# The first pairs of a squared-ReLU MLP: which sum's product comes first, where the low parts stand, and where the third pair's first product and its copy stand

## The chip, the core and the metric

The kernel runs on one core of a Trainium2 chip. The metric is the device time of one execution, in microseconds (us); lower is better. The core has a matrix engine (TensorE, PE in the profile), a vector engine (VectorE, DVE), a scalar engine (ScalarE, ACT), GpSimd (POOL) and SyncE (SP), which here only issues transfers. Each engine works through its own list of instructions; where one needs another's result it waits at that place in its list.

## What is computed

One layer of a diffusion trunk for 640 tokens (128 of a prompt, 512 latent) of width 1024: a token mixer with three head groups, then an MLP. The change lies in the MLP's first half:

```python
x = _layernorm(ALPHA * x + g1 * m, lp['ln1_g'], lp['ln1_b'])
hid = jnp.square(jax.nn.relu((x * (1.0 + sc2) + sh2) @ lp['w_ff1']))
x = _layernorm(ALPHA * x + g2 * (hid @ lp['w_ff2']), lp['ln2_g'], lp['ln2_b'])
```

`w_ff1` is 1024 x 4096 in float32. Rounding has to stay near that of float32, so every operand is split into a rounded high part and a low part (what is left), and a product of two operands is three matmuls: high by high, high by low, low by high.

## The kernel before

**The tiling.** The 4096 hidden columns are worked in 16 pairs (`u` = 0 to 15) of 256. A pair is a 2 x 2 product of blocks: the tokens in two halves of 320 (`HALF`), the 1024 inputs in two halves of 512, the hidden columns in two blocks of 128. Instead of eight block products the kernel forms seven, with sums of blocks on either side (Winograd's form): `m1` = a11 b11, `m2` = a12 b21, `m6` = s2 t2, `m5` = s1 t1, `m7` = s3 t3, `m4` = a22 t4, `m3` = s4 b22. The a's are the four quarters of the modulated, transposed input (`raws`, tiles q00 to q11); s1 to s4 are sums of quarters and are formed once, in the first pairs. The b's are quarters of a pair's weights and t1 to t4 their sums (`b_sums3` and `b_sum4`, lines 1315, 1316 and 1320), formed anew for each pair. A product is 12 matmuls (`prod`, line 1461): four blocks of 128 inputs, three terms each.

**The results.** Products add up in PSUM: m1, m6, m7, m4 of a pair in its bank x, m2 in bank y, m5 and m3 in bank z. Between them ScalarE copies bank x aside, since each of its partial sums is used (`keep(u, 1)` after m1, `keep(u, 2)` after m6, `keep(u, 3)` after m7; line 1467). The next product into x can't begin before that copy has read the bank. `c11`, `c22`, `c21`, `c12` add a bank and a copy (`out_sum`, line 1480, VectorE) and apply the squared ReLU (`relu2`, lines 1472 and 1473 on ScalarE, line 1475 on VectorE).

**Splitting.** ScalarE rounds the high part and VectorE subtracts it for the low one: `hi_(u, what, lo, hi)` (line 1343) and `lo_` (line 1347) for weights, where what = 1 is b11, 2 is b21 and b22 (in that order), 3 is t1, t3, t2, t4 (in that order; `lo` and `hi` pick some of them); `sum_hi` (line 1284) and `sum_lo` (line 1287) for the a's and s's. The program's names in the profile are those of buffers: pairs alternate between two sets, and wf12h and wf12l are the even and the odd pair's b's, wf3h and wf3l the high and low parts of the t's, wf_t the t's before the split, wf_r the loaded weights.

**The order.** From the second half of the output projection on, the order of TensorE, ScalarE, VectorE and SyncE is written out by hand: each of them executes its instructions in the order in which the program text issues them. The lines ahead of the loop `for u in range(2, NU)` are such a list for the pairs 0 and 1 and the beginning of pair 2: m1(0) and m2(0) while the last 128 tokens are still normalized and transposed (`normalize(4)`, `turn(4)`, `h2(4, ...)`, lines 1279 and 1281 for the scaling), then m1(1), m2(1), the sums s1 and s2 and their splits, m6(0), m5(0), m6(1), m5(1), then s3, m7(0), m7(1), and so on to m3(1). In the loop of pair u stand, in this order: `m1(u)`, `keep(u, 1)`, the t's of pair u+1 (`b_sums`), `hi_(u+1, 1)`, m4 and m3 of pair u-1, `lo_(u+1, 1)`, the other splits of pair u+1 with `hi_(u+1, 3)` last, `m2(u)`, `c11(u)`, `m6(u)`, `keep(u, 2)`, `lo_(u+1, 3)`, `m5(u)`, `m7(u)`, `keep(u, 3)`. For u = 2 there is no m4 and m3 of pair 1 (they stand in the list ahead).

**Loads.** `load(u)` reads a pair's weights by SyncE into one of two tiles, w0 and w1, once the tile's former reader is done; s1 (`s1r`) and s2 (`s2r`) lie in these two tiles at first, so load(2) waits for the last reader of `s1r` and load(3) for that of `s2r`. Finished blocks of hidden values are parked in DRAM by GpSimd (`store`).

Of the kernel before, what the change touches and what calls it, by code (L numbers as in the profile page):

```python
# [33 lines left out]
HALF = NTOK // 2  # L34
# [23 lines left out]
def f32(ap):  # L58
    return ap.bitcast(F32)
# [3 lines left out]
def hybrid_layer_kernel(ctx: ExitStack, tc: tile.TileContext, T):  # L63
    nc = tc.nc
    V, A, G, PE = nc.vector, nc.scalar, nc.gpsimd, nc.tensor
# [928 lines left out]
    gr, parts, tok, wks = {}, {}, {}, {}  # L994
# [203 lines left out]
    def parts(*names):  # L1198

        for n in names:  # L1200
            t = sps.tile([P, 2, 4, HALF], F32R, tag=n, name=n)
            sums[n] = [t[:, 0], t[:, 1]]
# [59 lines left out]
    def turn(t, bank="f", qs=(0, 1)):  # L1262

        for q in qs:
            pst[t, q] = fps[0].tile([P, 512], F32, tag=bank, name=f"psh{t}{q}")
            for k in range(4):
                kk = q * 4 + k
                PE.transpose(pst[t, q][:, k * P : (k + 1) * P], xn[:, t, kk * P : (kk + 1) * P], ident)

    def h2(t, q, *which):  # L1270

        v = 1 if t == 0 else 0
        spans = ((0, 64, 0, 256), (64, 64, 1, 0)) if t == 2 else ((0, P, t // 3, t * P - t // 3 * HALF),)
        for o, n, th, c0 in (spans[i] for i in which or range(len(spans))):
            for k in range(4):
                kk = q * 4 + k
                dst, src = raws[th, q][:, k, c0 : c0 + n], pst[t, q][:, k * P + o : k * P + o + n]
                if q and t:
                    V.tensor_scalar(dst, src, a2[:, kk, v : v + 1], b2[:, kk, v : v + 1], op0=ALU.mult, op1=ALU.add)
                else:  # L1280
                    A.activation(dst, src, AF.Identity, scale=a2[:, kk, v : v + 1], bias=b2[:, kk, v : v + 1])

    def sum_hi(n, src, lo=0, hi=HALF):
        A.copy(sums[n][0][:, :, lo:hi], src[:, :, lo:hi])

    def sum_lo(n, src, lo=0, hi=HALF):
        V.tensor_tensor(sums[n][1][:, :, lo:hi], src[:, :, lo:hi], f32(sums[n][0][:, :, lo:hi]), op=ALU.subtract)
# [18 lines left out]
    def b_sums(u, pool, tag):  # L1306

        b_sums3(u, pool, tag)
        b_sum4(u)

    def b_sums3(u, pool, tag):
        g = U[u]
        r = g.r
        g.t = t = pool.tile([P, 4, 4, P], F32, tag=tag, name=f"wf_t{u}")
        V.tensor_tensor(t[:, 0:2], r[:, :, :, 1, :], r[:, 0].rearrange("p k c n -> p c k n"), op=ALU.subtract)
        V.tensor_tensor(t[:, 2], r[:, 1, :, 1, :], t[:, 0], op=ALU.subtract)

    def b_sum4(u):
        g = U[u]
        V.tensor_tensor(g.t[:, 3], g.r[:, 1, :, 0, :], g.t[:, 2], op=ALU.subtract)  # L1320
# [20 lines left out]
    def hi_(*a):  # L1341
        h, l, src = part(*a)
        A.copy(h, src)  # L1343

    def lo_(*a):
        h, l, src = part(*a)
        V.tensor_tensor(l, src, f32(h), op=ALU.subtract)  # L1347
# [22 lines left out]
    for t in range(NT):  # L1370
        ps = wo_gemm(t, 0, wk)
# [18 lines left out]
    for t in range(NT):  # L1390
        ps = wo_gemm(t, 1, wk, "y" if t == 4 else "f")
# [59 lines left out]
    def banks(u):  # L1451
        U[u].ps = {b: fps[0].tile([P, 512], F32, tag=b, name=f"ps{b}{u}") for b in "xy"}

    def prod(u, b, sn, wn, start):

        ps = U[u].ps[b][:, 0:HALF]
        sh, sl = sums[sn]
        wh, wl = U[u].w[wn]
        for k in range(4):
            for i, (a_, b_) in enumerate(((wh, sh), (wh, sl), (wl, sh))):  # L1460
                PE.matmul(ps, a_[:, k, :], b_[:, k, :], start=start and k == 0 and i == 0, stop=k == 3 and i == 2,  # L1461
                          skip_group_check=True)

    def keep(u, i):

        t = kept[:, (3 * u + i - 1) % 6, :]
        A.copy(t, U[u].ps["x"][:, 0:HALF])  # L1467
        setattr(U[u], f"s{i}", t)
# [14 lines left out]
    def m1(u):  # L1483
        prod(u, "x", "a11", "b11", True)

    def m2(u):
        prod(u, "y", "a12", "b21", True)

    def m6(u):
        prod(u, "x", "s2", "t2", False)  # L1490

    def m5(u):
        U[u].ps["z"] = fps[0].tile([P, 512], F32, tag="z", name=f"psz{u}")
        prod(u, "z", "s1", "t1", True)

    def m7(u):
        prod(u, "x", "s3", "t3", False)
# [4 lines left out]
    def m3(u):  # L1502
        prod(u, "z", "s4", "b22", False)
# [4 lines left out]
    def c22(u):  # L1508
        out_sum(u, "z", U[u].s3, 1, 1, False)
# [6 lines left out]
    def c12(u):  # L1516
        out_sum(u, "z", U[u].s2, 1, 0, True)
        store(u, 1)
# [20 lines left out]

    s1r, s2r, s3r = (wop.tile([P, 4, HALF], F32, tag=f"w{i}", name=f"s{i + 1}r") for i in range(3))  # L1540

    def sums12(lo, hi):
        c = slice(lo, hi)
        V.tensor_tensor(s1r[:, :, c], raws[1, 0][:, :, c], raws[1, 1][:, :, c], op=ALU.add)
        V.tensor_tensor(s2r[:, :, c], s1r[:, :, c], raws[0, 0][:, :, c], op=ALU.subtract)

    banks(0)
    banks(1)
    m1(0)
    turn(3, qs=(1,))  # L1550
    m2(0)
    h2(2, 0, 1)
    turn(3, qs=(0,))
    lo_(1, 1)
# [1 line left out]
    lo_(1, 2, 0, 1)  # L1556
    normalize(4, mvs[4])
    turn(4, "z")
    h2(3, 0)
    h2(4, 0)  # L1560
    h2(4, 1)
    m1(1)
    m2(1)
    keep(0, 1)
    keep(1, 1)
    sums12(0, 192)
    parts("s2")
    sum_hi("s2", s2r, 0, 192)
    hi_(1, 3, 2, 3)
    sums12(192, HALF)  # L1570
    sum_lo("s2", s2r, 0, 192)
    sum_hi("s2", s2r, 192)
    sum_lo("s2", s2r, 192)
    parts("s1")
    sum_hi("s1", s1r)
    sum_lo("s1", s1r)
    load(2, wop, "w0")
    lo_(1, 3, 2, 3)
    hi_(1, 3, 0, 2)
    hi_(1, 3, 3, 4)  # L1580
    hi_(1, 2, 1, 2)
    m6(0)
    keep(0, 2)
    m5(0)
    V.tensor_tensor(s3r, raws[0, 0], raws[1, 0], op=ALU.subtract)
    sums["s3"] = [rawp.tile([P, 4, HALF], F32R, tag=f"q{i}0", name=f"s3{i}") for i in range(2)]
    sum_hi("s3", s3r)
    lo_(1, 3, 0, 2)
    lo_(1, 2, 1, 2)
    m6(1)  # L1590
    keep(1, 2)
    m5(1)
    sum_lo("s3", s3r)
    lo_(1, 3, 3, 4)
    m7(0)
    parts("a22")
    sum_hi("a22", raws[1, 1])
    sum_lo("a22", raws[1, 1])
    hi_(2, 1)
    hi_(2, 2, 0, 1)  # L1600
# [16 lines left out]
    c22(1)  # L1617
    lo_(2, 1)
    m3(1)
    b_sums3(2, wop, "w2")  # L1620
    hi_(2, 3, 2, 3)
    lo_(2, 3, 2, 3)
    lo_(2, 2, 0, 1)
    c12(0)
    hi_(2, 3, 0, 2)
    c11(1)
    store(1, 0)
    lo_(2, 3, 0, 2)
# [3 lines left out]
    lo_(2, 3, 3, 4)  # L1632
    hi_(2, 2, 1, 2)
    lo_(2, 2, 1, 2)

    def pair(w, gh, gl, raw, rows_):

# [12 lines left out]
    for u in range(2, NU):  # L1650
        more = u + 1 < NU
        gate = None
        banks(u)
        if u + 2 < NU:
            load(u + 2, wop, f"w{u % 2}")
        elif more:
            raw0 = wop.tile([P, 2, 512], F32, tag="w0", name="wg0_r")
            ff2_raw(raw0, NF - 4, 0)
        m1(u)
        keep(u, 1)  # L1660
        if u > 2:
            c22(u - 1)
        if more:
            b_sums(u + 1, wop, "w2")
            hi_(u + 1, 1)
        else:
            early = sps.tile([P, 1024 + 2 * NTOK], F32, tag="a11", name="early")
            raw1 = early[:, 0:1024].rearrange("p (k n) -> p k n", n=512)
            ff2_raw(raw1, 0, 0)
            for i in range(2):  # L1670
                nc.sync.dma_start(early[:, 1024 + i * NTOK : 1024 + (i + 1) * NTOK], parked[i])
        if u > 2:
            m4(u - 1)
            c21(u - 1)
            m3(u - 1)
        if more:
            lo_(u + 1, 1)
            hi_(u + 1, 2)
            if u > 2:
                c12(u - 1)  # L1680
            lo_(u + 1, 2)
            hi_(u + 1, 3)
        else:
            c12(u - 1)

            f = f12[0].rearrange("p a k n -> p a (k n)")
            pair((f[:, 0:2], f[:, 2:4]), *(rows2(f3[0][i].rearrange("p a k n -> p (a k n)")) for i in range(2)), raw0, st[:, 0])
        m2(u)
        c11(u)
        m6(u)  # L1690
        keep(u, 2)
        if more:
            lo_(u + 1, 3)
            if 8 <= u < 12:
                gate = gate2(u - 8, f"w{(u + 1) % 2}")
        else:
            w1 = wop.tile([P, 4, 512], F32R, tag="w1", name="wg0_p")
            gs = [wop.tile([P, 2, NTOK], F32R, tag=f"w{i}", name=f"g0_{i}") for i in (2, 0)]
            pair((w1[:, 0:2], w1[:, 2:4]), *gs, raw1, rows2(early[:, 1024:]))
        m5(u)  # L1700
        m7(u)
        keep(u, 3)
        if gate:
            gate()
# [53 lines left out]
    for n in range(2):  # L1758
# [39 lines left out]
        for t in range(NT):  # L1798
# [5 lines left out]
            if n == 1:  # L1804
                nmu, rstd = mean_rstd(t, "b")
                for q in range(2):
                    sl = slice(q * 512, (q + 1) * 512)
                    V.scalar_tensor_tensor(xn[:, t, sl], xn[:, t, sl], nmu, l2[0][q], op0=ALU.add, op1=ALU.mult)
                for q in range(2):
                    sl = slice(q * 512, (q + 1) * 512)  # L1810
# [74 lines left out]
```

## Time and profile before

| | us |
|---|---|
| median of 3 runs | 931.95 |
| lowest, highest | 930.48, 932.97 |
| the profiled execution, its own time | 932.0 |
| its span in the trace | 930.2 |

The profile is of one execution. Its page gives each engine's busy time; other views list the same instructions by time (the timeline), by who waited for whom, by stretches (with the clock that TensorE was granted, 1.00 or 0.50 of 2.4 GHz), and as the chain of waits that ended last. A row of the timeline has start, duration, engine, line, operation, result and operands, number of instructions merged, and in brackets how long the engine had been idle and what released it. A line is that of a helper, so the rows are told apart by time and shape. In the trace the pairs' products run from 481 us to about 705 us.

### The profile page before, as it was taken

What the parts mean: (1) busy time and instruction counts of PE and PEld (TensorE: products, weight loads), DVE (VectorE), ACT (ScalarE), POOL (GpSimd) and SP (SyncE); (2) the same over time, 40 slices, a digit from 0 to 9 for tenths busy, and PEclk for the clock granted to TensorE, in tenths of its full rate; (3) what the DMA queues carried; (4) which work ended last, traced back from release to release, by engine and by line L of the source; (5) the groups of instructions that cost most, each with busy time, mean ns of one, the idle gap of its engine ahead of it and who ended that gap; (6) DMA issues with size and microseconds to landing.
All of it is one profiled execution on the core that took longest, in us unless ns stands there. A gap on an engine that the chain in (4) does not pass through costs nothing.

```text
span 930.2 us, 15406 instructions
## 1 busy us (share of the span) xinstructions
PE 878.0 (94%) x5941; PEld 760.8 (82%) x5941; DVE 663.0 (71%) x1228; ACT 475.9 (51%) x977; POOL 69.0 (7%) x136
## 2 busy tenths in 40 slices
PE   6989898999999998999999899999999999999996
PEld 3888796789889886677788799988998887888885
DVE  2379997988876878895789877676754837663448
ACT  3577666466654647852486545543553606243320
POOL 2200010210101010001000000011000000000000
PEclk9999998999999999999999999999999999999998
DMA  9961524432222202008102544455525835152202
GB/s 260 285 177 50 175 78 138 126 96 58 62 63 63 69 18 91 2 1 294 46 1 70 177 140 148 147 179 183 166 80 200 295 111 176 58 171 88 68 23 91
DMA packets 102314, 109.84 MB, mean 118 GB/s; under 512 B 6720, under 2 KB 82208, under 8 KB 102240
## 3 DMA queue, kind: packets, MB, share of 16 engines
q1 hardware_dynamic: 96256, 92.33, 32.0%
q0 software_dynamic: 5792, 16.44, 5.0%
q8 instruction: 47, 0.77, 0.4%
q14 instruction: 27, 0.22, 0.1%
q10 hardware_dynamic: 192, 0.08, 0.0%
HBM read 96.24 MB, written 12.58 MB: 117 GB/s over the span
## 4 chain that ended last, share of the span: by engine, by line
PE 70%; DVE 11%; DMA 8%; ACT 6%; issue 2%; SPq 1%; DVEq 0%; ACTq 0%
PE psx L1461 10%; PE psy L129 8%; PE psy L131 8%; PE psy L130 8%; PE psz L1461 5%; DMA wad<-in_w_ada 4%; PE psA L130 2%; PE psA L129 2%; PE psA L131 2%; PE psavA L731 2%; PE psy L1461 2%; DMA wf_r<-in_w_ff 2%; PE psavC L953 1%; DVE b_st L561 1%; PE pstA L721 1%
## 5 line engine op out<-in xcount | busy, mean ns | idle before, releaser
L92 DVE TENSOR_TENSOR gl<-hidb,gh 128x640 fp32r<-128x640 f32 x54 | 43.5, 821 | 59.2 <-ACT gh L91 59.2
L1461 PE MATMUL psx<-s,wf3h 128*128 128x320 f32 x256 | 58.6, 315 | 6.6 <-ACT kept L1467 4.5
L91 ACT CAST gh<-hidb 128x640 fp32r<-128x640 f32 x54 | 38.4, 727 | 48.9 <-PE psy L130 40.8
L129 PE MATMUL psA<-wa_h,xh 128*128 128x384 f32 x160 | 54.8, 344 | 0.0
L131 PE MATMUL psA<-wa_h,xl 128*128 128x384 f32 x160 | 54.4, 341 | 0.0
L130 PE MATMUL psA<-wa_l,xh 128*128 128x384 f32 x160 | 54.2, 340 | 0.0
L1467 ACT COPY kept<-psx 128x320 f32<-128x320 f32 x48 | 20.4, 428 | 59.7 <-PE psx L1461 59.7
L1461 PEld LDWEIGHTS psx<-s,wf3h 128*128 128x128 f32 x256 | 43.7, 192 | 7.6 <-ACT kept L1467 4.9
L1347 DVE TENSOR_TENSOR wf3l<-wf_t,wf3h 128x2048 fp32r<-128x2048 f32 (+2 forms) x20 | 37.3, 1864 | 8.2 <-ACT wf3h L1343 8.2
L1461 PE MATMUL psx<-s,wf3l 128*128 128x320 f32 x128 | 40.4, 316 | 0.0
L1343 ACT CAST wf3h<-wf_t 128x2048 fp32r<-128x2048 f32 (+2 forms) x20 | 30.9, 1552 | 5.4 <-DVE wf_t L1320 3.4
L1480 DVE TENSOR_TENSOR st<-psz,kept 128x320 f32<-128x320 f32 x32 | 15.7, 489 | 25.3 <-ACT kept L1467 12.8
L130 PE MATMUL pswo<-wo,mxh 128*128 128x512 f32 x80 | 31.4, 393 | 0.8 <-DVE wo L92 0.8
L129 PE MATMUL pswo<-wo,mxh 128*128 128x512 f32 x80 | 31.5, 396 | 0.5 <-ACT wo L91 0.4
L709 DVE TENSOR_REDUCE nmA<-pssA 128x1 f32<-128x768 f32 x32 | 30.2, 952 | 2.2 <-PE pssA L707 1.9
L129 PEld LDWEIGHTS psA<-wa_h,xh 128*128 128x128 f32 x160 | 30.1, 188 | 2.0 <-issue 1.2
L1527 POOL DMA_DIRECT2D hd<-st x28 | 15.3, 546 | 216.8 <-DVE st L1475 85.0
L131 PE MATMUL pswo<-wo,mxl 128*128 128x512 f32 x80 | 31.2, 390 | 0.0
L711 ACT ACTIVATE pA<-pssA,nmA 128x768 f32<-128x768 f32 x32 | 28.8, 903 | 3.4 <-DVE nmA L709 2.9
L130 PEld LDWEIGHTS psA<-wa_l,xh 128*128 128x128 f32 x160 | 30.2, 189 | 0.2
L131 PEld LDWEIGHTS psA<-wa_h,xl 128*128 128x128 f32 x160 | 30.1, 188 | 0.2
L1461 PE MATMUL psz<-s,wf3h 128*128 128x320 f32 x128 | 29.6, 318 | 0.0
(671 smaller groups left out, 2758.3 us busy)
## 6 DMA issues: line engine op xcount, KB each, us to landing
wad<-in_w_ada SPq DMA_DIRECT2D x32, 512.0 KB, 5.0
wf_r<-in_w_ff SPq DMA_DIRECT2D x32, 512.0 KB, 4.8
hd<-st POOLq DMA_DIRECT2D x28, 320.0 KB, 2.8
hidb<-hd SPq DMA_DIRECT2D x28, 320.0 KB, 4.7
adaw<-in_w_ada SPq DMA_DIRECT2D x32, 256.0 KB, 5.2
wa_r<-in_w_in SPq DMA_DIRECT2D x48, 128.0 KB, 2.7
wo_raw<-in_w_out SPq DMA_DIRECT2D x8, 512.0 KB, 6.5
x<-in_x_sample SPq DMA_DIRECT2D x8, 256.0 KB, 4.8
```

The source lines that it names most:

```text
L91: A.copy(hi, src)
L92: V.tensor_tensor(lo, src, f32(hi), op=ALU.subtract)
L129: PE.matmul(ps, s[0], m[0], start=start, stop=False)
L130: PE.matmul(ps, s[0], m[1], start=False, stop=False)
L131: PE.matmul(ps, s[1], m[0], start=False, stop=stop)
L709: V.tensor_reduce(nm, ps[:, 0:NKEY], axis=AX.X, op=ALU.max, negate=True)
L711: A.activation(pr, ps[:, 0:NKEY], AF.Exp, bias=nm, accum_out=sm[:, col : col + 1])
L731: PE.matmul(po, pT[:, c, :], vals(g, c, c0, n), start=(c == 0), stop=(c == NKC - 1))
L1343: A.copy(h, src)
L1347: V.tensor_tensor(l, src, f32(h), op=ALU.subtract)
L1461: PE.matmul(ps, a_[:, k, :], b_[:, k, :], start=start and k == 0 and i == 0, stop=k == 3 and i == 2, skip_group_check=True)
L1467: A.copy(t, U[u].ps["x"][:, 0:HALF])
```

## The change

- `h2`: of the last 128 tokens' second half, two of four scalings go from VectorE to ScalarE.
- `prod`: for pairs 0 and 1 the 12 matmuls are sorted so that those that read the low part of the a or s come last (eight, then four).
- `sums12` is divided into `sum1` and `sum2`; s1 is formed and split ahead of s2, and m5(0), m5(1) come ahead of m6(0), m6(1). The splits of pair 1's t's are placed anew: t1's go up ahead of the last tokens' work, t3's and b22's go behind m6(0) and m6(1).
- For pair 2, `banks(2)` and m1(2) stand ahead of its t's, `keep(2, 1)` stands behind `lo_(2, 2, 0, 1)`, and `hi_(2, 3, 0, 2)` goes ahead of `c12(0)`. `hi_(3, 1)` and `lo_(3, 1)` go from the loop to the end of the list, ahead of load(4) and `b_sums(3)`.

```diff
-                if q and t:
+                if q and t and not (t == 4 and k < 2):
...
-        for k in range(4):
-            for i, (a_, b_) in enumerate(((wh, sh), (wh, sl), (wl, sh))):
-                PE.matmul(ps, a_[:, k, :], b_[:, k, :], start=start and k == 0 and i == 0, stop=k == 3 and i == 2,
-                          skip_group_check=True)
+        terms = [(k, a_, b_) for k in range(4) for a_, b_ in ((wh, sh), (wh, sl), (wl, sh))]
+        if u < 2:
+            terms.sort(key=lambda v: v[2] is sl)
+        for i, (k, a_, b_) in enumerate(terms):
+            PE.matmul(ps, a_[:, k, :], b_[:, k, :], start=start and i == 0, stop=i == 11, skip_group_check=True)
...
     m2(0)
+    hi_(1, 3, 0, 1)
     h2(2, 0, 1)
...
     turn(4, "z")
+    lo_(1, 3, 0, 1)
     h2(3, 0)
     h2(4, 0)
     h2(4, 1)
     m1(1)
     m2(1)
+    sums12(0, 192)
+    parts("s1")
+    sum_hi("s1", s1r, 0, 192)
     keep(0, 1)
     keep(1, 1)
-    sums12(0, 192)
+    sum1(192, HALF)
+    sum_hi("s1", s1r, 192)
+    sum_lo("s1", s1r, 0, 192)
+    sum_lo("s1", s1r, 192)
+    m5(0)
+    sum2(192, HALF)
     parts("s2")
     sum_hi("s2", s2r, 0, 192)
+    sum_hi("s2", s2r, 192)
     hi_(1, 3, 2, 3)
-    sums12(192, HALF)
     sum_lo("s2", s2r, 0, 192)
-    sum_hi("s2", s2r, 192)
     sum_lo("s2", s2r, 192)
-    parts("s1")
-    sum_hi("s1", s1r)
-    sum_lo("s1", s1r)
+    m5(1)
     load(2, wop, "w0")
     lo_(1, 3, 2, 3)
-    hi_(1, 3, 0, 2)
-    hi_(1, 3, 3, 4)
-    hi_(1, 2, 1, 2)
     m6(0)
     keep(0, 2)
-    m5(0)
     V.tensor_tensor(s3r, raws[0, 0], raws[1, 0], op=ALU.subtract)
     sums["s3"] = [rawp.tile([P, 4, HALF], F32R, tag=f"q{i}0", name=f"s3{i}") for i in range(2)]
+    hi_(1, 3, 1, 2)
     sum_hi("s3", s3r)
-    lo_(1, 3, 0, 2)
-    lo_(1, 2, 1, 2)
     m6(1)
     keep(1, 2)
-    m5(1)
+    lo_(1, 3, 1, 2)
+    hi_(1, 2, 1, 2)
+    lo_(1, 2, 1, 2)
     sum_lo("s3", s3r)
-    lo_(1, 3, 3, 4)
+    hi_(1, 3, 3, 4)
     m7(0)
     parts("a22")
     sum_hi("a22", raws[1, 1])
+    lo_(1, 3, 3, 4)
     sum_lo("a22", raws[1, 1])
...
     m3(1)
+    banks(2)
+    m1(2)
     b_sums3(2, wop, "w2")
     hi_(2, 3, 2, 3)
     lo_(2, 3, 2, 3)
     lo_(2, 2, 0, 1)
+    keep(2, 1)
+    hi_(2, 3, 0, 2)
     c12(0)
-    hi_(2, 3, 0, 2)
...
     lo_(2, 2, 1, 2)
+    hi_(3, 1)
+    lo_(3, 1)
...
-        banks(u)
+        if u > 2:
+            banks(u)
...
-        m1(u)
-        keep(u, 1)
         if u > 2:
+            m1(u)
+            keep(u, 1)
             c22(u - 1)
         if more:
             b_sums(u + 1, wop, "w2")
+        if more and u > 2:
             hi_(u + 1, 1)
-        else:
+        if not more:
...
         if more:
-            lo_(u + 1, 1)
+            if u > 2:
+                lo_(u + 1, 1)
             hi_(u + 1, 2)
```

## Rows read from the trace of the kernel before

**Rows 1.** The page: busy time, share of the span and instructions of each engine

```profile
PE 878.0 (94%) x5941; PEld 760.8 (82%) x5941; DVE 663.0 (71%) x1228; ACT 475.9 (51%) x977; POOL 69.0 (7%) x136
```

**Rows 2.** Stretches: length, busy PE, PEld, DVE, ACT, POOL (instructions), TensorE clock, DMA, GB/s

```profile
481.00:526.50 45.50, 37.84 (x234) 36.60 (x233) 39.81 (x62) 29.35 (x53) 2.17 (x4) 0.92 0.29 99
530.00:592.00 62.00, 62.00 (x425) 62.00 (x424) 45.44 (x57) 31.79 (x51) 5.40 (x10) 1.00 0.41 140
```

**Rows 3.** Who waited for whom, 481 to 527: us in total, times, longest

```profile
PE psx L1461 <- ACT kept L1467: 4.5, 1, 4.5
...
PE psx L1461 <- ACT s L1284: 1.8, 1, 1.8
```

**Rows 4.** Chain of waits, 486 to 540: start, us, what; TensorE's products on it

```profile
521.25 2.93 PE psx L1461 x12
524.18 2.39 PE psz L1461 x12
...
532.05 1.76 PE psz L1461 x12
```

**Rows 5.** Stretches around TensorE's gaps, columns as in rows 2

```profile
485.80:486.80 1.00, 0.00 (x0) 0.00 (x0) 1.00 (x4) 1.00 (x2) 0.00 (x0) 1.00 0.03 8
...
495.00:498.00 3.00, 3.00 (x13) 3.00 (x13) 3.00 (x4) 1.85 (x5) 0.00 (x0) 0.50 0.25 67
...
522.10:525.40 3.30, 3.30 (x15) 3.30 (x14) 3.23 (x5) 1.75 (x2) 0.00 (x0) 0.50 0.93 291
```

**Rows 6.** Timeline of ScalarE, first products

```profile
483.20 1.29 ACT L1281 ACTIVATE q<-psh,b,a 128x64 f32<-128x64 f32 x4 [1.33 <-PE psx L1461]
...
486.67 2.89 ACT L1281 ACTIVATE q<-psh,b,a 128x128 f32<-128x128 f32 x8
489.40 0.79 ACT L1467 COPY kept<-psx 128x320 f32<-128x320 f32 x2
491.21 0.83 ACT L1284 CAST s<-s2r 128x768 fp32r<-128x768 f32 x1 [1.01 <-DVE s2r L1545]
...
497.88 1.26 ACT L1284 CAST s<-s3r 128x1280 fp32r<-128x1280 f32 x1 [0.66 <-DVE s3r L1585]
501.00 0.43 ACT L1467 COPY kept<-psx 128x320 f32<-128x320 f32 x1 [1.86 <-PE psx L1461]
```

**Rows 7.** Timeline of VectorE, same time

```profile
487.95 1.37 DVE L1279 TENSOR_SCALAR q<-psh,a,b 128x128 f32<-128x128 f32 x4 [0.69 <-PE psh L1268]
...
499.50 1.49 DVE L1287 TENSOR_TENSOR s<-s3r,s 128x1280 fp32r<-128x1280 f32 x1
...
502.62 1.49 DVE L1287 TENSOR_TENSOR a<-q,a 128x1280 fp32r<-128x1280 f32 x1 [1.04 <-ACT a L1284]
```

**Rows 8.** Timeline of ScalarE, pair 2's first products

```profile
515.08 0.47 ACT L1472 ACTIVATE st<-st 128x320 f32<-128x320 f32 x1 [1.76 <-DVE st L1480]
...
518.88 0.62 ACT L1343 CAST wf3h<-wf_t 128x512 fp32r<-128x512 f32 x1 [1.89 <-DVE wf_t L1320]
...
520.28 0.60 ACT L1343 CAST wf12h<-wf_r 128x512 fp32r<-128x512 f32 x1
...
524.22 1.90 ACT L1343 CAST wf3h<-wf_t 128x2048 fp32r<-128x2048 f32 x1 [1.55 <-DVE wf_t L1320]
526.03 0.42 ACT L1467 COPY kept<-psx 128x320 f32<-128x320 f32 x1
```

**Rows 9.** Timeline of VectorE, same time

```profile
517.02 1.23 DVE L1347 TENSOR_TENSOR wf3l<-wf_t,wf3h 128x1024 fp32r<-128x1024 f32 x1 [1.05 <-ACT wf3h L1343]
...
520.91 0.69 DVE L1347 TENSOR_TENSOR wf12h<-wf_r,wf12h 128x512 fp32r<-128x512 f32 x1 [0.69 <-ACT wf12h L1343]
521.52 1.22 DVE L1315 TENSOR_TENSOR wf_t<-wf_r 128x1024 f32<-128x1024 f32 x1
...
524.10 1.82 DVE L1347 TENSOR_TENSOR wf12l<-wf_r,wf12l 128x512 fp32r<-128x512 f32 x2
```

**Rows 10.** Timeline of all engines: the weight load with which m7(2) begins

```profile
526.50 0.30 PEld L1461 LDWEIGHTS psx<-s,wf3h 128*128 128x128 f32 x2 [0.18 <-ACT kept L1467]
```

More of the change, by code (lines that the diff above doesn't have):

```diff
@@ L1540, in hybrid_layer_kernel, with sum1, sum2, sums12 @@
     s1r, s2r, s3r = (wop.tile([P, 4, HALF], F32, tag=f"w{i}", name=f"s{i + 1}r") for i in range(3))
-    def sums12(lo, hi):
+    def sum1(lo, hi):
         c = slice(lo, hi)
         V.tensor_tensor(s1r[:, :, c], raws[1, 0][:, :, c], raws[1, 1][:, :, c], op=ALU.add)
+    def sum2(lo, hi):
+        c = slice(lo, hi)
         V.tensor_tensor(s2r[:, :, c], s1r[:, :, c], raws[0, 0][:, :, c], op=ALU.subtract)
+    def sums12(lo, hi):
+        sum1(lo, hi)
+        sum2(lo, hi)
     banks(0)
```

## Prediction

> **What bounds the kernel now.** I read the page first: TensorE is busy 94% of the span [rows 1]. That is an average, so I went on to the stretches. In the steady part of the pairs, 530 to 592, TensorE has no idle time at all, at full clock, while VectorE has some 17 us to spare [rows 2]; there a pair costs seven products of 1.76 us [rows 4], 12.3 us. In the stretch that the change touches, 481 to 526.5, TensorE is busy 37.84 of 45.50 us at a mean clock of 0.92, and VectorE is the busier engine, 39.81 us [rows 2]. So at most about 10 us are to be had: 7.7 of idle time and what the low clock costs. Whatever TensorE's place is when pair 2's m7 begins is carried to the end: behind it the products run without a gap, and loads and stores are released by work that moves with them.
>
> The waits name the two large gaps: 4.5 us in which m6(2) waits for the copy keep(2,1), and 1.8 us in which m6(0) waits for the high part of s2 [rows 3]. The change goes for both. The row that decides, though, is a small one: m7(2) starts at 526.50 after 0.18 us of waiting for *another* copy, keep(2,2) [rows 10]. That copy ran at 526.03, behind the 1.90 us high part of pair 3's t's (`hi_(3, 3)`, 524.22), which had itself waited 1.55 us for VectorE's last t sum [rows 8]. ScalarE works in program order, and in the list keep(2,2) stands behind `hi_(3, 3)` before and after. So m7(2) is already held by the two elementwise engines, and the time that m6(2) waits ahead of it is cover, not cost. The question is whether the change makes that elementwise chain earlier.
>
> **The change, part by part.** Durations are of the rows; the next instruction on ScalarE or VectorE starts some 0.08 us before the listed end of an independent one, and a waiter starts about 0.05 after the end that it waits for.
>
> *First sum first.* t1 of pair 1 is rounded in the 1.33 us in which ScalarE waits ahead of 483.20 [rows 6], and its low part is subtracted in VectorE's 0.69 us ahead of 487.95 [rows 7]; both cost nothing (0.62 and 0.69 without that cover). ScalarE does 8 scalings in 2.89 us from 486.67 [rows 6], 0.36 each; two more bring it to 490.33. Then the first part of s1's high part (0.75), the two copies (0.70) and the second part (0.62; prices by 491.21, 489.40 and 518.88) [rows 6, 8] end at 492.39. m5(0) starts at 492.44, where the first product after m2(1) starts at 493.21 now (491.4 plus 1.8). VectorE, two scalings shorter, has s1 ready before. The low part of s1 follows at 493.1, in time for the sorted order, whose first eight matmuls don't need it. Four products then run unbroken, 492.44 + 4 x 1.76 = 499.48. In the kernel before they lose time to the second wait and to the half clock of 495 to 498 [rows 5] and end at 502.57. On TensorE alone that is a gain of 3.1 us.
>
> *Where it goes.* In the new list keep(0,2) stands ahead of the high parts of t3 and s3, and it must wait for the end of the *third* product, 492.44 + 3 x 1.76 + 0.2 = 497.95. Queued behind it on ScalarE: t3 (498.3), s3 (1.26 us, 498.85 to 500.1), keep(1,2), and b22 of pair 1 (to 501.0). VectorE has the low part of b22 (0.69) ahead of that of s3 and waits for it, so `sum_lo("s3")` starts at 501.65, against 499.50 now [rows 7], and `sum_lo("a22")`, behind t4's, at 503.66, against 502.62: 1.04 us *later*. m7(0) waits 0.7 us for s3's high part and, after its eight first matmuls, 1.85 us for the low one (503.2). From there on VectorE's order is that of the kernel before, and nearly all of its stretch hangs on itself, so s4, c11(0), c22(0), c22(1) and pair 2's first t's are all 1.04 late. TensorE reaches m1(2) at 513.5, where it was before (513.1).
>
> *Pair 2.* Moving `hi_(2, 3, 0, 2)` ahead of c12(0) takes that one's two passes on ScalarE (515.08 and its like, 0.88 us) [rows 8] out of its way; keep(2,1), now ahead of it, has to wait for the end of m1(2), 515.5. `hi_(2, 3, 0, 2)` then starts at 515.9 (515.96 now), and its low part at 516.97, against 517.02 [rows 9]. The 1.04 us are paid back here, no more. t4's sum, c12(1) and b22's high and low part keep their order and times (low part 520.9 in both) [rows 9]. Then `lo_(3, 1)` stands ahead of `b_sums(3)`, where it stood behind it: 0.69 us for this shape, part of the 1.82 us pair at 524.10 now, less the overlap: 0.6 us [rows 9]. So the t's of pair 3 start at 522.1 (521.52 now), `hi_(3, 3)` at 524.85, keep(2,2) at 526.65, and m7(2) at 527.1: **0.6 us later** than now. SyncE's load(2) goes out some 2 us earlier, load(3) 1 us later; both land well ahead of their first use, and load(4) waits for the same low part of b22 as before: nothing.
>
> Meanwhile m6(2) does start early, at 517.25 for 521.25 now, and m5(2) ends at 520.9. The 4.5 us wait isn't removed; it stands before m7(2) instead, 6.2 us long.
>
> *TensorE's clock.* After the gap that ended at 521.25, the clock fell to half, 1.2 GHz, and stayed there past 525.4 [rows 5]; the 24 matmuls of m6(2) and m5(2) took 2.93 + 2.39 = 5.32 us [rows 4] for 3.52 at full clock, 1.6 us too long without the 0.18 of waiting. Now this lies beside the wait for keep(2,2) and costs nearly nothing. In the changed kernel the matmuls that follow the gap are m7(2), m1(3) and so on, with nothing beside them. Bounds: nothing if the clock holds, 2.2 us if it stays low a third longer after the longer gap. I take **1.5 us**, the price of [rows 4] nearly whole.
>
> The Trainium skill ("TensorE: Matmul & The Clock Gate", section on HAM oscillation) says that a matmul kernel pays for a re-throttle after each long enough wait, not only once. It speaks against this change, which leaves TensorE five waits where there were three, the last of them longer. By its formula, throttled time times one half, a low stretch of 3.3 us [rows 5] would be an estimated 1.65 us for each such wait; the trace agrees for the last one [rows 4], but after the shortest gap of now the clock held [rows 5], so I charge one wait, not each.
>
> **The sum**, against the profiled execution (932.0, span 930.2; the median of the runs is 931.95, so it stands for them): +0.6 for the chain, +1.5 for the clock, 934.1; rounded to **934.0**. The rows differ by some tenths from my steps, and 20 waits add up, so the chain's end is good to about 0.6 either way.
>
> **The rivals.**
> - *The clock isn't exposed.* The low stretch could end within the wait. Then +0.6 alone: 932.6. Against it: both gaps of over 2 us were followed by one [rows 5]. Chance 0.17.
> - *Slower: the clock falls already at m5(0).* TensorE is idle from 491.2 to 492.44. After the 1.0 us gap of 485.8 it kept 1.00; after the 2.6 us stretch with one lone matmul it fell [rows 3, 5]. 1.2 us is nearest to the first, so I count no fall. But if it falls there, three products at half clock push the end of m6(0) out by up to 1.6 us, and with it keep(0,2), s3, a22, s4 and all of VectorE's chain up to m7(2): 935.6. The point that decides is the granted clock between 492.4 and 497.7. The waits of 0.7 and 1.85 us at m7(0) are of the same kind, but a fall behind them costs the chain only about 0.6. Together 0.22.
> - *Faster: the copy isn't held.* Had keep(2,2) no more to wait for than m6(2), m7(2) would follow m5(2) at 520.9, at full clock, 5.6 us earlier than now: 926.4. For it: the change's two large gaps are what the waits show. Against it: the order on ScalarE, and VectorE, which would have to be 5 us earlier in a stretch in which it is busy 88% of the time. Chance 0.06; with part of it (a chain 1 us or more earlier than I count, and no clock loss) 0.09.
> - *The change doesn't do what it says* holds for one piece: m1(2) isn't earlier on TensorE, as it followed m3(1) directly already. Only its copy moves; that is in the sum.
>
> **How the numbers follow.** Forecast 0.52, 932.9 to 935.0; clock hidden 0.17; slower rival 0.22; faster 0.09. The range leaves out the faster case and the far end of the slower one, and takes in half a microsecond of chain and the runs' own spread of about 1 us: 931.2 to 935.8. About 0.3%, 2.8 us, is what a measurement of this kernel can tell from no change. Slower by that, over 934.75: the slower rival and a fifth of the forecast, 0.32. Faster, under 929.15: 0.08. Within: 0.60.
>
> **What would show it.** In the changed kernel's trace: m5(0) near 492.4 and no half clock before 498; `sum_lo("s3")` near 501.6 after a wait for b22's high part; m7(0) cut in two by a wait of nearly 2 us; m6(2) near 517.3 directly after m2(2); then a gap of some 6 us that keep(2,2) ends, m7(2) near 527.1, and behind it 3 us or so at clock 0.50. Wrong if m7(2) starts before 525.5, if ScalarE's `hi_(3, 3)` doesn't stand before keep(2,2), or if the time behind m7(2) changes in another way than by the clock.

## The result, and the profile after

The changed kernel took 939.9 us (median), the kernel before 932.46 in the runs beside it; the ratio is 1.0069, interval 1.0048 to 1.0089. It is slower by 6.4 us, where 2.1 were forecast; the range ended at 935.8. Two runs at a lower granted clock, 1074.85 us in a3 and 974.88 us in b6 below, are left out of the times and the ratios.

The page of the changed kernel; TensorE's share of the span is what it was [rows 1]:

```profile
PE 881.7 (94%) x5941; PEld 763.9 (81%) x5941; DVE 662.4 (70%) x1228; ACT 476.4 (51%) x981; POOL 69.0 (7%) x136
```

Its span is 940.0 us, 9.8 longer, but 2.9 of that are there before the changed stretch begins: the transposes of the last 128 tokens (`turn(4)`) start at 486.81 before and at 489.75 after. Ahead of that point the change only sorts the matmuls of m1(0) and m2(0) and puts the rounding of t1 there, and in the traces of the kernels below `turn(4)` lies anywhere between 486.3 and 490.5; b2, b4 and b7, whose edits lie behind it, have it at 487.85, 489.39 and 490.02. So that shift is the run's, not the change's, and places are compared from `turn(4)` on. From there to the start of m2(3), the last product before the steady rhythm, it is 47.00 us before and 53.28 after: 6.28 us, close to the measured 6.4. The 0.6 us that are left of the 9.8 lie behind it.

Stretches of the changed kernel (length, busy PE, PEld, DVE, ACT, POOL, TensorE clock, DMA, GB/s):

```profile
484.00:533.20 49.20, 36.77 (x234) 35.00 (x232) 39.70 (x63) 30.12 (x57) 2.18 (x4) 0.95 0.27 92
545.00:590.00 45.00, 45.00 (x309) 45.00 (x308) 32.84 (x41) 22.42 (x35) 3.78 (x7) 1.00 0.42 145
494.30:497.00 2.70, 0.06 (x1) 0.00 (x0) 2.67 (x4) 2.05 (x5) 0.00 (x0) 1.00 0.00 0
498.50:501.00 2.50, 2.50 (x12) 2.50 (x11) 2.50 (x4) 1.14 (x2) 0.00 (x0) 0.50 0.48 134
527.00:533.00 6.00, 0.14 (x1) 0.00 (x0) 5.86 (x9) 3.52 (x5) 0.33 (x1) 0.91 0.70 229
533.30:538.00 4.70, 4.70 (x18) 4.70 (x19) 2.56 (x3) 0.43 (x1) 0.00 (x0) 0.50 0.66 216
```

The steady pairs are as before [rows 2]. Ahead of them TensorE stands idle 12.4 of 49.2 us; two gaps, near 494 to 497 and 527 to 533, are each followed by a stretch at half clock. In the second one the clock fell before the matmuls resumed (0.91 on average in it).

Who waited for whom, 484 to 534 (us in total, times, longest); before, there were 4.5 and 1.8 us [rows 3]:

```profile
PE psx L1463 <- ACT kept L1468: 6.7, 2, 6.1
...
PE psz L1463 <- ACT s L1284: 2.7, 1, 2.7
...
DVE q L1279 <- ACT q L1281: 2.4, 1, 2.4
...
PE psx L1463 <- DVE s L1287: 1.5, 1, 1.5
```

The third line is new and was in no step of the prediction: VectorE's scaling waits for ScalarE's. On the chain of waits it stands first (start, us, what):

```profile
489.69 3.50 ACT q L1281 x10
493.21 0.73 DVE q L1279 x2
493.94 0.88 DVE s1r L1545
...
497.11 5.32 PE psz L1463 x24
502.43 1.77 PE psx L1463 x12
504.23 0.43 ACT kept L1468
504.65 0.52 ACT wf3h L1343
505.17 1.16 ACT s L1284
...
530.95 1.90 ACT wf3h L1343
532.85 0.33 ACT kept L1468
533.23 8.04 PE psx L1463 x36
541.27 1.76 PE psz L1463 x12
```

From above: ten scalings on ScalarE, then VectorE's two, then s1. m5(0) and m5(1), 24 matmuls, take 5.32 us, at half clock in part. keep(0,2) waits for the third product, and t3 and s3 are queued behind it. At the end `hi_(3, 3)`, keep(2,2), and m7(2), m1(3), m4(2), 36 matmuls, in 8.04 us. Before, the chain has for the same 36:

```profile
526.58 5.48 PE psx L1461 x36
```

Two rows of VectorE's and TensorE's timeline, for the two places:

```profile
493.21 0.73 DVE L1279 TENSOR_SCALAR q<-psh,a,b 128x128 f32<-128x128 f32 x2 [2.42 <-ACT q L1281]
```

```profile
533.23 0.90 PE L1463 MATMUL psx<-s,wf3h 128*128 128x320 f32 x2 [6.09 <-ACT kept L1468]
```

The second row is the wait that the forecast moved from m6(2) to m7(2), there at 6.2 us, found at 6.09.

The sum, from `turn(4)`: m7(2) starts 39.69 us behind it before [rows 10] and 43.48 after, 3.8 later, where 0.6 was forecast; the 36 matmuls then cost 2.5 us more than before, where 1.5 was forecast. 3.8 + 2.5 = 6.3.

### The profile page after: what moved, and what is told of

Read it like the earlier page. It is cut to its first block, busy times and chain, and to the rows that moved or that the text cites. A ratio compares the mean times of both kernels' runs of the same rounds, so it can differ in the third digit from the quotient of the medians.

```text
span 940.0 us, 15414 instructions
## 1 busy us (share of the span) xinstructions
PE 881.7 (94%) x5941; PEld 763.9 (81%) x5941; DVE 662.4 (70%) x1228; ACT 476.4 (51%) x981; POOL 69.0 (7%) x136
## 4 chain that ended last, share of the span: by engine, by line
PE 67%; DVE 12%; DMA 9%; ACT 8%; issue 3%; SPq 2%; DVEq 0%; ACTq 0%
PE psx L1463 9%; PE psy L130 7%; PE psy L129 7%; PE psy L131 7%; PE psz L1463 5%; DMA wad<-in_w_ada 4%; PE psA L130 2%; PE psA L129 2%; PE psA L131 2%; PE psavA L731 2%; PE psy L1463 2%; DMA wf_r<-in_w_ff 2%; PE psavC L953 1%; DVE b_st L561 1%; PE pstA L721 1%
```

## The experiments

Two theories stood at the start. **The split theory:** VectorE waited because both engines were to read one PSUM bank; s1 came 1.7 us late, TensorE's gap ahead of m5(0) was 2.75 us instead of the forecast 1.2, its clock fell, and m6(0), keep(0,2) and all behind it were late by both. The rest is as forecast. **Its rival:** the chain of pairs 0 and 1 is late on its own, by the new order of the sums, and the low clock came by chance. The forecast's own mechanism (keep(2,2) behind `hi_(3, 3)`, and the uncovered half clock) was tested beside them. All ratios are to the kernel before on the same chip; 0.001 is 0.93 us. "Stage" is the time from `turn(4)` to m2(3) in the run's trace, as a difference from before.

| kernel | ratio, 95% interval | stage, us |
|---|---|---|
| changed | 1.0069, 1.0048 to 1.0089 | +6.3 |
| a1: scalings not divided | 1.0022, 1.0006 to 1.0039 | +2.8 |
| a5: divided, two PSUM banks | 1.0023, 1.0003 to 1.0042 | +2.6 |
| a6: matmuls in the first gap | 1.0036, 1.0020 to 1.0053 | +4.9 |
| a4: matmuls in the last gap | 1.0022, 1.0008 to 1.0035 | +3.8 |
| a2: copy ahead of the rounding | 1.0013, 0.9995 to 1.0031 | +1.0 |
| a3: a1 and a2 | 0.9958, 0.9943 to 0.9973 | -2.3 |
| b1: a3 and a later keep(0,2) | 0.9954, 0.9942 to 0.9967 | -4.5 |
| b6: b1, copy still higher | 0.9961, 0.9945 to 0.9976 | -3.2 |
| b2: before, pair 2's part alone | 1.0028, 1.0013 to 1.0044 | +2.5 |
| b3: before, the first pairs' part alone | 1.0064, 1.0051 to 1.0077 | +4.3 |
| b4: before, divided scalings alone | 1.0048, 1.0026 to 1.0069 | +3.1 |
| b7: before, copy ahead alone | 0.9995, 0.9981 to 1.0009 | +0.2 |

**The division undone (a1).**

```diff
-                if q and t and not (t == 4 and k < 2):
+                if q and t:
```

> The changed kernel with one piece undone: all four scalings of the last 128 tokens' second half are on VectorE again. Theory A (two engines read one PSUM bank, so VectorE's two scalings wait for ScalarE's ten; s1 comes 1.7 us late, TensorE's gap ahead of m5(0) grows from 1.2 to 2.8 us and its clock falls): the wait of 2.4 us on VectorE is gone, m5(0) starts 1.7 us earlier against the start of normalize(4), no clock of 0.50 in m5(0) and m5(1), m7(2) 3.3 us earlier; 6 us gap and low clock at m7(2) remain; about 936.6. Rival B (the split is harmless, the clock fell for another reason): m7(2) at its old place, about 939.9.

Measured: 935.95 us. TensorE's starts after a gap, and its products on the chain:

```profile
496.14 0.41 PE L1463 MATMUL psz<-s,wf3h 128*128 128x320 f32 x1 [1.05 <-ACT s L1284]
...
530.72 0.90 PE L1463 MATMUL psx<-s,wf3h 128*128 128x320 f32 x2 [6.09 <-ACT kept L1468]
```

```profile
496.14 3.78 PE psz L1463 x24
...
530.72 7.77 PE psx L1463 x36
```

The gap ahead of m5(0) is 1.05 us, and its 24 matmuls run at full clock (3.78 for 5.32 us). m7(2) starts 40.25 us behind `turn(4)` (530.72 less 490.47), 0.56 later than before; the forecast had 0.6. So the division makes s1 late, and with this one piece away the kernel does what was forecast of the whole: 2.1 us slower. That it does so by the bank is not shown yet.

**One bank or two (a5).** Is it the bank? The four transposes whose scaling is divided go to two banks, two each, and nothing else changes.

```diff
+            if t == 4 and q:
+                pst[5, 1] = fps[0].tile([P, 512], F32, tag="f", name="psh51")
             for k in range(4):
                 kk = q * 4 + k
-                PE.transpose(pst[t, q][:, k * P : (k + 1) * P], xn[:, t, kk * P : (kk + 1) * P], ident)
+                to = pst[5, 1] if t == 4 and q and k < 2 else pst[t, q]
+                PE.transpose(to[:, k * P : (k + 1) * P], xn[:, t, kk * P : (kk + 1) * P], ident)
...
-                dst, src = raws[th, q][:, k, c0 : c0 + n], pst[t, q][:, k * P + o : k * P + o + n]
+                dst, src = raws[th, q][:, k, c0 : c0 + n], pst[5 if t == 4 and q and k < 2 else t, q][:, k * P + o : k * P + o + n]
```

> The changed kernel, but the four transposes whose scaling is divided go into two PSUM banks: ScalarE reads its two blocks from one, VectorE its two from the other. Theory A (VectorE waited because both engines were to read one bank): the 2.4 us wait is gone, s1 comes some 2.3 us earlier, m5(0) waits for 1.2 us or less, its clock holds, m7(2) some 3.3 us earlier than in the changed kernel, as with the split undone; about 936. Rival B (VectorE waits because of the tile that both write, or ScalarE is simply first in some order): the wait stays and the time is near 939.9.

Measured: 935.06 us. VectorE's timeline has no wait ahead of the two scalings now, and m5(0) and m5(1) run at full clock:

```profile
489.35 0.73 DVE L1282 TENSOR_SCALAR q<-psh,a,b 128x128 f32<-128x128 f32 x2
490.00 0.95 DVE L1548 TENSOR_TENSOR s1r<-q,q 128x768 f32<-128x768 f32 x1
```

```profile
493.60 3.79 PE psz L1466 x24
```

m7(2) stands 39.96 us behind `turn(4)`, 3.5 earlier than in the changed kernel, where 3.3 were expected. Both engines still write the same tile of the input's quarter; only the PSUM tile that they read differs. So the wait goes with what is read, not with what is written. That PSUM tile fills a bank (128 x 512 float32), and no run has two tiles in one bank, so tile and bank aren't told apart. The wait itself is put there by the program: the traces of the changed kernel, a6 and b4 have a semaphore instruction of VectorE's at the line of the scaling (at 490.9 in the changed kernel), and those of a1, a3 and a5 have none. The Trainium skill ("PSUM — Partial Sum Buffer", section on PSUM bank collisions) gives a reason for such a wait: two engines that access one bank and the same partitions at a time collide, a read beside a read included, and a compiler's scheduler adds dependencies for it by bank and group of 32 partitions, not by address. The trace agrees as to the wait, 2.42 us with one bank and none with two; a collision no run here shows.

**Wait and clock told apart (a6).** 16 matmuls, their results unused, behind m2(1) of the changed kernel:

```diff
     m2(1)
+    filler = fps[0].tile([P, 512], F32, tag="f", name="filler")
+    for i in range(16):
+        PE.matmul(filler[:, 0:HALF], U[1].w["b21"][0][:, i % 4, :], sums["a12"][0][:, i % 4, :], start=True, stop=True)
     sums12(0, 192)
```

> The changed kernel with 16 added matmuls (results unused) behind m2(1), which fill 2.3 us of TensorE's 2.75 us gap ahead of m5(0). Theory A (of the 3.3 us by which m7(2) came later than forecast, 1.7 are VectorE's wait and 1.6 the half clock after it): m5(0) starts where it did, its clock stays at 1.00, m7(2) is 1.5 us earlier; about 938.2. Rival B (the wait alone makes the chain late, the low clock is beside other work): 939.9, or later by what the added matmuls push out.

Measured: 936.68 us. VectorE's wait is still there, and m5(0) starts where it did, 7.37 us behind `turn(4)` (7.36 in the changed kernel), but at full clock:

```profile
495.88 3.79 PE psz L1463 x24
...
530.46 8.19 PE psx L1463 x36
```

m7(2) comes 41.95 us behind `turn(4)`, 1.53 earlier than in the changed kernel. So of the 3.2 us by which m7(2) missed the forecast, 1.5 are the clock's at m5(0) and 1.7 the wait's. The whole kernel's ratio is lower too, but the two intervals overlap a little, so this step rests on the traces.

**The last gap filled (a4).** The changed kernel with 36 matmuls between m5(2) and m7(2):

```diff
         m5(u)
+        if u == 2:
+            filler = fps[0].tile([P, 512], F32, tag="f", name="filler")
+            for i in range(36):
+                PE.matmul(filler[:, 0:HALF], U[u].w["t1"][0][:, i % 4, :], sums["s1"][0][:, i % 4, :], start=True, stop=True)
         m7(u)
```

> The changed kernel with 36 added matmuls (results unused, into a free PSUM bank) between m5(2) and m7(2), so that TensorE works through most of the 6.1 us gap. Theory A (the half clock after the gap costs 2.5 us, for nothing lies beside it): m7(2) starts at the same place, the clock behind it stays at 1.00, m7(2), m1(3) and m4(2) take 5.3 instead of 8.0 us; 937.4 although 5.3 us of work were added. Rival B (the low clock is hidden or has another reason): 939.9 or more.

Measured: 935.23 us, faster than expected.

```profile
532.54 0.55 PE L1463 MATMUL psx<-s,wf3h 128*128 128x320 f32 x2 [0.81 <-ACT kept L1468]
```

```profile
532.54 5.54 PE psx L1463 x36
```

m7(2) starts 43.48 us behind `turn(4)`, to the hundredth as in the changed kernel; the 36 matmuls behind it take 5.54 instead of 8.04 us. The half clock after the gap costs 2.5 us, and nothing covers it.

**The copy ahead of the rounding (a2), and with a1 (a3).** For pair 2, m2, m6 and keep(2,2) are issued ahead of `hi_(3, 3)`:

```diff
             lo_(u + 1, 2)
+            if u == 2:
+                m2(u)
+                m6(u)
+                keep(u, 2)
             hi_(u + 1, 3)
...
-        m2(u)
+        if u > 2:
+            m2(u)
         c11(u)
-        m6(u)
-        keep(u, 2)
+        if u > 2:
+            m6(u)
+            keep(u, 2)
```

> The changed kernel with m2(2), m6(2) and keep(2,2) issued ahead of hi_(3,3), for pair 2 alone. Theory A (the copy is held by the 1.9 us rounding that waits for VectorE's t sums): the 6.1 us gap ahead of m7(2) shrinks to below 2.5 us, the clock behind it stays at 1.00, m4(2) ends about 6 us earlier; 933.7. Rival B (the copy is not what holds m7(2), or VectorE holds the next product as long): the same gap stands before m7(2) or m4(2); 938 or more.

> Both of the edits before: no split of the scalings, and the copy ahead of the rounding. Theory A (two separate causes that add): 3.3 + 6.2 us off the changed kernel, 930.4. Rival B (they overlap, as TensorE alone sets the end once the copy is free): 932 to 934.

Measured: 934.23 and 929.52 us. TensorE's starts after a gap in a2:

```profile
525.69 0.56 PE L1463 MATMUL psx<-s,wf3h 128*128 128x320 f32 x2 [1.71 <-ACT kept L1468]
530.08 0.56 PE L1463 MATMUL psx<-a,wf3h 128*128 128x320 f32 x2 [0.60 <-ACT kept L1468]
532.49 2.03 PE L1463 MATMUL psz<-s,wf12h 128*128 128x320 f32 x12 [0.38 <-DVE st L1481]
```

The 6.1 us gap is 1.7, the clock behind it stays at 1.00, and the stage is 5.3 us shorter than the changed kernel's. With the division undone as well it is shorter by 8.6 (3.5 of a1 plus 5.3 of a2 is 8.8): the causes are separate and add. a3 beats the kernel before by 0.4%.

**The parts alone on the kernel before (b2, b3, b4, b7).** b2 has the third pair's part of the diff, b3 the rest of it, b4 the `h2` line alone, b7 a2's edit. The lines of b2 ahead of the loop (those in it are as in the change), and that of b4:

```diff
     m3(1)
+    banks(2)
+    m1(2)
     b_sums3(2, wop, "w2")
...
     lo_(2, 2, 0, 1)
+    keep(2, 1)
+    hi_(2, 3, 0, 2)
     c12(0)
-    hi_(2, 3, 0, 2)
...
     lo_(2, 2, 1, 2)
+    hi_(3, 1)
+    lo_(3, 1)
```

```diff
-                if q and t:
+                if q and t and not (t == 4 and k < 2):
```

> The kernel before with the third pair's part of the change alone: m1(2), keep(2,1), hi_(2,3,0,2) and the splits of b11 of pair 3 moved, pairs 0 and 1 as before. Theory A (it moves the wait from m6(2) to m7(2), about as long, and uncovers the half clock): a 6 us gap ahead of m7(2), which starts within 0.5 us of its place before, then 0.50 clock; 2.3 us slower than before, about 935.3. Rival B (with the older first part the chain is early enough): faster than before by 1 to 5 us.

> The changed kernel with the third pair's part undone: first sum first, low parts last and the split of the scalings stay. Theory A (the first part makes VectorE's chain 1.0 us later by keep(0,2), 1.7 by the split's wait and 1.6 by the clock at m5(0), and pair 2's wait covers the second low clock): m7(2) 4.2 us later than before, at full clock soon after; 936.7 to 937.5. Rival B (the chain's delay is taken back by the older order of pair 2): within 1 us of before.

> The kernel before with the divided scalings alone. Theory A (the wait for ScalarE's ten scalings is a cost by itself): VectorE waits 2.4 us more, s1 and s2 come 1.7 us later, the gap ahead of m6(0) grows to 3.5 us, and m7(2) comes some 1.5 us later; 934.2. Rival B (pair 2's long wait covers it): within 0.5 us of before.

> The kernel before with keep(2,2), m2(2) and m6(2) ahead of hi_(3,3), and nothing else. Theory A (before, m6(2) itself is late by keep(2,1), so that keep(2,2) has little to gain): m7(2) 0.2 to 0.7 us earlier, time within 1 us of before. Rival B (the copy's place is the whole matter, with or without the change): 4 us faster.

Measured: 935.21, 938.46, 937.13 and 932.73 us. TensorE's start of m7(2) in b2 and of m6(2) in b3 and b7, one row each:

```profile
527.62 0.90 PE L1461 MATMUL psx<-s,wf3h 128*128 128x320 f32 x2 [6.26 <-ACT kept L1467]
```

```profile
527.49 0.80 PE L1463 MATMUL psx<-s,wf3h 128*128 128x320 f32 x2 [4.83 <-ACT kept L1468]
```

```profile
524.47 0.90 PE L1461 MATMUL psx<-s,wf3h 128*128 128x320 f32 x2 [4.46 <-ACT kept L1467]
```

b2 is the moved wait by itself: m7(2) stands 39.77 us behind `turn(4)`, 0.1 later than before, after a gap of 6.26 us, and the half clock behind it makes the stage 2.5 us longer. b3 keeps the old wait at m6(2) and is late by the first pairs' chain: m7(2) is 4.25 us later than before, where 4.2 were expected. b4 cost more than expected, 3.1 us in the stage and 4.5 by its ratio for 1.5: VectorE's wait was 3.0 us there, TensorE's gap ahead of m6(0) 3.48, and the low clocks after both gaps ran longer than before. b7 gives nothing: before, m6(2) itself waits until 521.25 for keep(2,1) [rows 3, 4], so the place of keep(2,2) matters only once that wait is gone; m7(2) is 0.3 us later than before, where 0.2 to 0.7 earlier were expected. So keep(2,1) up costs and keep(2,2) up does nothing, each alone; where keep(2,1) is up already, keep(2,2) up takes 5.3 us (a2) or 5.1 us (a3 against a1) off the stage. No run has these two moves and nothing else.

**Further along (b1, b6).** b1 is a3 with keep(0,2) behind the high parts that were queued on it; b6 moves m2(2), m6(2) and keep(2,2) up once more, from ahead of `hi_(3, 3)` to ahead of `hi_(3, 1)` (only the added lines are shown).

```diff
     m6(0)
-    keep(0, 2)
     V.tensor_tensor(s3r, raws[0, 0], raws[1, 0], op=ALU.subtract)
...
     hi_(1, 3, 1, 2)
+    hi_(1, 2, 1, 2)
     sum_hi("s3", s3r)
+    hi_(1, 3, 3, 4)
+    keep(0, 2)
     m6(1)
     keep(1, 2)
     lo_(1, 3, 1, 2)
-    hi_(1, 2, 1, 2)
     lo_(1, 2, 1, 2)
     sum_lo("s3", s3r)
-    hi_(1, 3, 3, 4)
```

```diff
     lo_(2, 2, 1, 2)
+    m2(2)
+    m6(2)
+    keep(2, 2)
     hi_(3, 1)
     lo_(3, 1)
```

> The run with both edits (no split, copy of m6(2) ahead of the rounding of pair 3's t's), and keep(0,2) behind the high parts of t3, b22, s3 and t4 of pair 1. Theory A (keep(0,2), which waits for the third product, holds ScalarE and with it VectorE some 3 us): VectorE's wait ahead of t3's low part is gone, m7(0) starts unbroken, the chain up to m7(2) is 2 to 3 us earlier; 927.5. Rival B (the next in line takes its place: the copies, or TensorE itself, are as late): 929 to 930, as without this edit.

> The run with three edits (no split, late keep(0,2), copy ahead), but keep(2,2), with m2(2) and m6(2), stands ahead of hi_(3,1) too, not only ahead of hi_(3,3). Theory A (the 1.7 us that are left ahead of m7(2) are the roundings of pair 3's b's): that gap goes to 0.3 us or less and the time falls by 1 to 1.7 us, to about 926.8. Rival B (the next copy or the sum c22(2) is as late): the gap moves to m4(2) or m3(2) and the time stays at 928.3.

Measured: 928.31 and 929.21 us. In b1 the wait of m7(0) for s3 is gone and the stage is 2.2 us shorter than in a3; by the ratios the two can't be told apart. It beats the kernel before by 0.46% (interval 0.33 to 0.58) and the changed one by over 1%. In b6 the gap only moves, to m4(2):

```profile
521.03 0.57 PE L1463 MATMUL psx<-s,wf3h 128*128 128x320 f32 x2 [0.23 <-ACT kept L1468]
527.12 0.56 PE L1463 MATMUL psx<-a,wf3h 128*128 128x320 f32 x2 [2.29 <-ACT kept L1468]
```

That is keep(2,3), which is queued behind `hi_(3, 3)` in its turn. In b1 the rest of the gap lies in three pieces of 1.71, 0.60 and 0.38 us and the clock held; here it is one of 2.29, and the clock fell 0.9 us after it.

## Why the prediction was wrong

**The step that failed** is in "First sum first": "VectorE, two scalings shorter, has s1 ready before". Any wait of VectorE's was put at nothing there. The step weighed the scalings by the engines' time alone. VectorE's two were not beside ScalarE's ten but behind them (2.42 us of waiting), so s1 was late, not early, and the division that was to shorten VectorE's list by 0.7 us lengthened the chain by 1.7. a1 and a5 show it from two sides. I had no row in which two engines share the reading of one bank, and the term should have had two bounds: nothing if they overlap, the whole ScalarE group if they don't.

**The rival that came true** is the slower one, the clock falling at m5(0), but by this cause. I had set the point of decision rightly, the clock between 492.4 and 497.7 (`turn(4)` plus 5.6 to 10.9), and its price, 1.6 us, was measured at 1.53 (a6). Its chance hung on a gap of 1.2 us; with that gap (1.05 us in a1) the clock held, with 2.75 it fell.

**What was right.** The moved wait: m7(2) held by keep(2,2) behind `hi_(3, 3)`, 6.2 us forecast, 6.09 found, and the cause shown by a2. The chain's +0.6 us, found as 0.56 where the division is undone (a1) and 0.27 where it is kept without the wait (a5). In a1 the steps behind it hold too, so it isn't luck: the high part of pair 2's first t is 1.03 us late (1.04 forecast), `lo_(2, 3, 0, 2)` is back at its old place (0.05 early), and pair 3's t's start 0.56 late (0.6 forecast). `sum_lo("s3")` behind b22's high part and m7(0) cut in two (1.54 us of waiting, 1.85 forecast). Load(2), load(3) and load(4): no wait of TensorE for them in the stage.

**The term that was mis-sized** is the clock behind the last gap: 1.5 us taken, 2.2 as the upper bound, 2.3 to 2.7 measured (7.77 to 8.19 us for 36 matmuls, against 5.48 on the chain of before). I took the price from one gap of 4.45 us, after which the first matmuls still ran at full speed and the fall came 0.8 us later:

```profile
521.25 0.56 PE L1461 MATMUL psx<-s,wf3h 128*128 128x320 f32 x2 [4.45 <-ACT kept L1467]
```

After 6.1 us the first two matmuls already took 0.90 us, and all the matmuls at half clock stood where they set the end. The gap's length alone doesn't explain the difference: behind the same gap the first two took 0.90 us in b4 and b7 as well, and the 24 matmuls of m6(2) and m5(2) took 5.93 and 5.70 us there, for 5.32 before. One trace gave one case of the price, and it was a cheap one. The sum with the measured terms is 0.6 + 1.7 + 1.5 + 2.5 = 6.3 us.

## What to carry to other kernels

Before work is divided between two engines, look at what both would read: here two engines that were to read one PSUM bank ran one behind the other, and the half that was to be hidden then set the end; with two banks the division cost nothing. When a wait is moved out of an engine's way, find the next thing queued in front of what it waits for, in the in-order engine that releases it: here one copy was raised and the next one, 6 us later, took its place, while raising both gained 0.4% over the kernel before, with the division undone (a3). The long gaps in TensorE's work had a second price here, the half clock behind them, and what counted was whether the matmuls after the gap had a wait beside them. A price that is read from one gap in one trace is one case, not a bound.

## What the runs showed of the hardware

Adding matmuls whose results nobody uses shortened the stage, twice: 36 of them in a 6.1 us gap by 2.5 us, 16 in a 2.75 us gap by 1.4. In the stage's traces TensorE's clock stayed at 1.00 around single gaps of 0.23 to 1.71 us, and fell in or after those of 2.29 to 6.26 us. In the kernel before it fell after 1.78 and 0.41 us with one matmul between them. How much a fall costs isn't fixed by the gap: behind gaps of 6.08 to 6.26 us the same 36 matmuls took 7.77 (a1), 7.91 (a5), 8.04 (changed), 7.99 (b2) and 8.19 us (a6). Nor is its moment: in the kernel before, the clock was 1.00 through the 4.45 us gap ahead of m6(2) and fell 0.8 us behind its end; in the same gap of b7 (4.46 us) it was 0.72 on average, having fallen inside.
